# Three layers of a two-block transformer step in another order

## The chip, the cores and the metric

The kernel runs on one core of one Trainium2 chip. The metric is the device time of one execution in microseconds (us). Engines are named as the profile names them: PE (TensorE), PEld (its weight loads), DVE (VectorE), ACT (ScalarE), POOL (GpSimd), SP (SyncE, which only issues transfers here).

## What is computed

256 tokens of width 1024 go through two blocks, all in float32. Cut to what matters:

```
x = x + sliding_window_attention(norm(x))     # "SWA": 16 query heads, 4 key heads, window 128, sinks
x = x + swiglu_ffn(norm(x))                   # "FFN 1"
x = norm(x)
x = x + ab_mixer(norm(x))                     # "AB": a recurrence over tokens, both directions, 4 heads,
                                              #   beside a gated spatial mix, one output projection
x = x + relu2_ffn(norm(x))                    # "FFN 2a"
x = x + latent_attention(norm(x), positions)  # "MLA": 16 heads, low-rank queries and keys, rope
x = x + relu2_ffn(norm(x))                    # "FFN 2b"
return norm(x)

# the recurrence of one head and direction (h_fwd, h_bwd): out = num / max(|den|, exp(-m)),
# num and den from exp-weighted causal sums of q k v
ha = rms_norm(h_fwd + h_bwd, head_g) * sigmoid(o)
# the spatial mix: hb = gelu(u) * (rms_norm(gelu(v), v_g) mixed over tokens by ws, + bs)
# softmax attention of SWA: p = exp(s - m); out = (p / sum p) v
```

## The kernel before

All weights come as one stream of units of 128 x 1024 floats, two to a transfer of 1 MB (`raw`). Each unit is split before use into a high part (`wh`, ACT, line 262) and a rest (`wl`, DVE, line 263); activations are split in the same way (`hb`, `xb`: ACT lines 311 and 314, DVE lines 312 and 315). A product of two split operands is three matmuls: high with high, rest with high, high with rest. A unit is split when its turn in the program comes (`load`, by `self.ahead` and `self.limit`), and a transfer is issued when the buffer of the pair three before it has been read.

The code is written in program order, and a scheduler then sets each engine's queue by it; `high_priority`, `issue_after` and `keep_in_program_order` move single instructions. Each engine works through its queue in order, so an instruction that waits holds all behind it.

In SWA, pair j of heads goes through `proj(j)` (query projection), `soft(j)` (scores on PE; bias, maximum `swm`, exponentials, normalisation `sws` on DVE and ACT), `trans(j)` (the weights transposed on PE, copied to `swpt` by ACT) and `value(j)` (8 matmuls of 64 columns, then a split into `hb`). `out_steps` gives the output projection as steps (n, kp): column half n, and the k-th two pairs kp, 12 matmuls of 512 columns each. Steps (0, 0) to (0, 3) are interleaved with the last `trans` and `value` by `hooks`.

AB's recurrence (`ab_heads`) runs stages by a string: o (projection of the output gate), w (`weights`: decay by exp on ACT into `mex`, masked by POOL, times the scores on DVE), n (`numer`: numerator and denominator, `mden`, `mh`), b (projection of the spatial branch). ACT's functions come from several tables, and each change of table is an ACT_TABLE_LOAD. `uproj(m)` projects the third branch.

MLA projects to latents (`lck`, `lcq`), makes keys `kT` (`mla_keys`, two halves), queries per four heads (`rope(g)`, `nope(g)`), values (`values(n)`), and per head `soft(h)`, `trans(h)` (copy to `mpt`), and per two heads `value(j)`, which are laid out in a loop over heads, again with output steps among the last.

`boundary` adds the result to x and transposes it for the next stage (`x_trans`).

## Time and profile before

| | us |
|---|---|
| median of 3 runs (lowest to highest) | 849.87 (849.39 to 851.83) |
| the profiled execution, its own time | 851.47 |
| its span in the trace | 849.8 |
| SWA, to the first matmul of FFN 1 proper | 0 to 88.4 |
| AB, heads of the recurrence to its output projection | 317 to 362.9 |
| MLA, to the first matmul of FFN 2b | about 561 to 662.4 |

The span is what the trace covers, and the execution's own time holds 1.7 us around it. Times of day in the text (64.76) are us from the span's start.

### The profile page before, as it was taken

Reading aid. Unit: us, or ns where it says so; the run is one execution under the profiler, and the core shown is the slowest. Engines: PE = TensorE matmul, PEld = TensorE weight load, DVE = VectorE, ACT = ScalarE, POOL = GpSimd, SP = SyncE. Lnnn points to the kernel's source line nnn. Section 1 sums busy time; section 2 is a strip of 40 time slices with the busy share of each in tenths; the row PEclk is TensorE's granted clock in tenths of the full one; section 3 lists DMA queues with packets and bytes.
Section 4 is the critical chain, followed back from the end, with each engine's and each line's share of the span. In section 5 each row is a group of like instructions: output and inputs, shape, how many; then the busy total and the mean of one; then the engine's idle time right before and its main releaser. Section 6 shows DMA issues by size and latency. Waiting matters only on the chain.

```text
span 849.8 us, 12664 instructions
## 1 busy us (share of the span) xinstructions
PE 835.0 (98%) x4768; PEld 721.3 (85%) x4768; DVE 606.6 (71%) x1135; ACT 510.5 (60%) x972; POOL 41.5 (5%) x58
## 2 busy tenths in 40 slices
PE   9999999999999999999999999999999999999996
PEld 9877888888888987988888888898877888888885
DVE  5897776666766897787666766667878766666644
ACT  6696655555455969866455645456787744545532
POOL 0520000000000002200000000001000000000001
PEclk9999999999999999999999999999999999999999
DMA  9447555555554514554655555545217655555511
GB/s 328 173 163 263 179 208 191 196 180 179 196 199 148 199 51 149 199 205 148 220 184 195 195 198 197 195 169 173 85 51 245 219 206 199 198 184 175 190 47 49
DMA packets 24109, 151.41 MB, mean 178 GB/s; under 512 B 2768, under 2 KB 3536, under 8 KB 6768
## 3 DMA queue, kind: packets, MB, share of 16 engines
q1 hardware_dynamic: 23712, 149.95, 49.8%
q8 instruction: 37, 0.61, 0.3%
q10 hardware_dynamic: 288, 0.52, 0.2%
q0 software_dynamic: 48, 0.13, 0.1%
q14 instruction: 24, 0.20, 0.1%
HBM read 149.03 MB, written 1.05 MB: 177 GB/s over the span
## 4 chain that ended last, share of the span: by engine, by line
PE 78%; DVE 10%; ACT 6%; DMA 3%; issue 2%; POOL 1%; SPq 0%; POOLq 0%; DVEq 0%; ACTq 0%
PE ps L293 76%; DVE wl L263 3%; DMA raw<-in_w_dram 3%; PE ps L303 2%; ACT wh L262 1%; DMA x<-in_x_dram 1%; DVE qk L888 1%; DVE xb L315 1%; DVE sws L723 1%; ACT mpr L1291 1%; DVE sws L704 1%; ACT L890 0%; DVE qT L1259 0%; POOL r L319 0%; ACT mex L994 0%
## 5 line engine op out<-in xcount | busy, mean ns | idle before, releaser
L263 DVE TENSOR_TENSOR wl<-raw,wh 128x1024 fp32r<-128x1024 f32 (+4 forms) x278 | 329.3, 1190 | 134.8 <-ACT wh L262 128.9
L262 ACT ACTIVATE wh<-raw 128x1024 fp32r<-128x1024 f32 (+4 forms) x278 | 284.2, 1032 | 136.3 <-PE ps L293 123.0
L293 PE MATMUL ps<-xb,wh 128*128 128x512 f32 (+1 forms) x1304 | 283.5, 356 | 1.2 <-ACT wh L262 0.7
L293 PE MATMUL ps<-wh,hb 128*128 128x512 f32 (+1 forms) x944 | 280.3, 379 | 0.3 <-ACT hb L311 0.3
L293 PEld LDWEIGHTS ps<-xb,wh 128*128 128x128 f32 x1304 | 215.6, 189 | 32.9 <-DVE xb L315 1.6
L293 PEld LDWEIGHTS ps<-wh,hb 128*128 128x128 f32 x944 | 169.1, 189 | 31.9 <-issue 1.7
L293 PE MATMUL ps<-wl,hb 128*128 128x512 f32 (+1 forms) x472 | 177.6, 377 | 0.5 <-DVE wl L263 0.5
L293 PE MATMUL ps<-xb,wl 128*128 128x256 f32 x1084 | 159.3, 282 | 0.0
L293 PEld LDWEIGHTS ps<-xb,wl 128*128 128x128 f32 x1084 | 150.5, 191 | 9.4
L311 ACT ACTIVATE hb<-fp 128x256 fp32r<-128x256 f32 x90 | 36.9, 415 | 119.2 <-DVE fp L545 89.7
L293 PEld LDWEIGHTS ps<-wl,hb 128*128 128x128 f32 x472 | 88.8, 188 | 17.3 <-DVE wl L263 0.9
L312 DVE TENSOR_TENSOR hb<-fp,hb 128x256 fp32r<-128x256 f32 x90 | 37.7, 424 | 33.9 <-ACT hb L311 33.9
L447 DVE TENSOR_TENSOR fg<-ps,fg 128x256 f32<-128x256 f32 x108 | 44.6, 417 | 10.4 <-ACT fg L446 10.4
L446 ACT ACTIVATE fg<-ps 128x256 f32<-128x256 f32 x108 | 39.9, 369 | 11.1 <-PE ps L293 11.0
L293 PE MATMUL ps<-wh,xb 128*128 128x512 f32 (+3 forms) x192 | 39.8, 350 | 0.0
L293 PEld LDWEIGHTS ps<-wh,xb 128*128 128x128 f32 x192 | 31.6, 189 | 3.5
L319 POOL TENSOR_TENSOR r<-ms,mhalf 128x2 f32<-128x2 f32 x7 | 5.3, 760 | 485.4 <-DVE ms L324 485.4
L545 DVE SCALAR_TENSOR_TENSOR fp<-fg 128x256 f32<-128x256 f32 x64 | 26.8, 423 | 1.8
L314 ACT ACTIVATE xb<-ps,cols 128x256 fp32r<-128x256 f32 x35 | 15.5, 470 | 18.8 <-PE ps L303 12.9
L315 DVE SCALAR_TENSOR_TENSOR xb<-ps,cols,xb 128x256 fp32r<-128x256 f32 x35 | 16.0, 479 | 9.6 <-ACT xb L314 9.5
L293 PE MATMUL ps<-wl,xb 128*128 128x512 f32 (+3 forms) x96 | 21.4, 348 | 0.0
L1291 ACT ACTIVATE mpr<-ps,mnm,qsc 128x256 f32<-128x256 f32 x32 | 17.8, 574 | 4.3 <-DVE mnm L1287 4.2
(224 smaller groups left out, 611.0 us busy)
## 6 DMA issues: line engine op xcount, KB each, us to landing
raw<-in_w_dram SPq DMA_DIRECT2D x135, 1024.0 KB, 4.7
raw<-in_w_dram SPq DMA_DIRECT2D x4, 512.0 KB, 7.2
xraw<-in_xt_dram SPq DMA_DIRECT2D x4, 257.0 KB, 4.9
raw<-in_w_dram SPq DMA_DIRECT2D x4, 256.0 KB, 5.6
x<-in_x_dram SPq DMA_DIRECT2D x4, 256.0 KB, 6.5
row_fn<-in_fn_dram SPq DMA_DIRECT2D x2, 512.0 KB, 6.2
kT<-kr SPq DMA_DIRECT2D x1, 512.0 KB, 4.6
out_dram<-fo SPq DMA_DIRECT2D x2, 256.0 KB, 2.0
```

The lines of the kernel that those rows point to most:

```text
L262: a = self.nc.scalar.activation(hi[:, c], raw[:, c], AF.Copy)
L263: b = self.nc.vector.tensor_tensor(out=lo[:, c], in0=raw[:, c], in1=hi[:, c].bitcast(F32), op=ALU.subtract)
L293: self.nc.tensor.matmul(out, lhsT, rhs, start=start, stop=stop)
L303: self.nc.tensor.transpose(out, in_, self.ident)
L311: self.last_act = nc.scalar.activation(hi, src, AF.Copy)
L312: self.last_dve = nc.vector.tensor_tensor(out=lo, in0=src, in1=hi.bitcast(F32), op=ALU.subtract)
L314: self.last_act = nc.scalar.activation(hi, src, AF.Copy, scale=scale)
L315: self.last_dve = nc.vector.scalar_tensor_tensor(out=lo, in0=src, scalar=scale, in1=hi.bitcast(F32), op0=ALU.mult, op1=ALU.subtract)
L446: self.nc.scalar.activation(out, ps[:, T:], AF.Copy)
L447: self.nc.vector.tensor_tensor(out=out, in0=ps[:, :T], in1=out, op=ALU.add)
L545: nc.vector.scalar_tensor_tensor(out=p, in0=g, scalar=0.0, in1=g, op0=ALU.max, op1=ALU.mult)
L1291: nc.scalar.activation(pr[:, t], s3[:, t], AF.Exp, scale=qsc[:, t : t + 1], bias=nm[:, t : t + 1], accum_out=den[:, t : t + 1])
```

## The change

Three layers are reordered. In SWA, values are taken in twos (0 and 1 after `soft(4)`, 2 and 3 after `soft(6)`, and so on), there are six buffers `swpt` in place of four, and the end is written as `late`, with the step (1, 0) of the second column half ahead of values 6 and 7. In AB, sigmoid, exponentials and gelu wait for the last function of the table before (`issue_after`), the gate comes after w3, the multiplication by `head_g` goes from POOL into the split of `hh`, parts of `weights` and `numer` get priority, and `uproj(3)` is ahead of the transposes. In MLA, queries' `rope(0)` and `nope(0)` come ahead of the second half of the keys, values in twos after heads 7, 11 and 15, the weight units are split earlier and more evenly over the heads (`split`), and the end is again a `late` with steps of both column halves. The order of units in the stream follows.

```diff
@@ order of the output weights in the stream
+SWA_OUT = ((0, 0), (0, 1), (0, 2), (1, 0), (0, 3), (1, 1), (1, 2), (1, 3))
+MLA_OUT = ((0, 0), (0, 1), (1, 0), (0, 2), (1, 1), (0, 3), (1, 2), (1, 3))
...
@@ second_weights: latent attention
+            u.append(keys[0])
             for g4 in range(4):
...
                 if g4 == 0:
+                    u.append(keys[1])
                     u += wv
...
@@ def swa
-                pt = self.t([P, 3 * P], "swpt", 4)
+                pt = self.t([P, 3 * P], "swpt", 6)
...
-        hooks = {
-            1: lambda: (trans(6), value(5)),
-            2: lambda: (trans(7), value(6)),
-            3: lambda: value(7),
-        }
-        steps, accs = self.out_steps(acts, hooks)
+        steps, accs = self.out_steps(acts, {})
         for i in range(8):
             self.ahead = max(3, i - 1)
             proj(i)
@@ -761,14 +765,27 @@
                 soft(i - 1)
             if i >= 3:
                 trans(i - 3)
-            if i >= 4:
+            if i in (5, 7):
+                value(i - 5)
                 value(i - 4)
-        steps[0].pop(0)()
+        steps[0][0]()
         soft(7)
         trans(5)
-        value(4)
         self.pin = False
-        return self.boundary(steps, accs, lambda: None, nextw)
+
+        def late():
+            steps[0][1]()
+            trans(6)
+            value(4)
+            value(5)
+            steps[0][2]()
+            trans(7)
+            steps[1][0]()
+            value(6)
+            value(7)
+            steps[0][3]()
+
+        return self.boundary(([late], steps[1][1:]), accs, lambda: None, nextw)
...
@@ the ab layer
-        self.hg = self.row("hg")
...
-            nc.scalar.activation(y, y, AF.Silu)
+            self.last_silu = nc.scalar.activation(y, y, AF.Silu)
...
-        nc.scalar.activation(em, ac[:, :, 64:100], AF.Exp, scale=-1.0)
+        with self.tc.issue_after(self.last_silu.ins):
+            nc.scalar.activation(em, ac[:, :, 64:100], AF.Exp, scale=-1.0)
...
+                with self.tc.issue_after(self.last_silu.ins):
+                    for b, c0, cw, _, cb in segs:
+                        self.last_exp = nc.scalar.activation(exf[:, c0 : c0 + cw], bp[:, cb : cb + cw], AF.Exp, scale=-1.0, bias=ac[:, b, rr : rr + 1])
...
-                for b, c0, cw, cs, _ in segs:
-                    nc.vector.scalar_tensor_tensor(out=exf[:, c0 : c0 + cw], in0=sps[:, cs : cs + cw], scalar=P ** -0.5, in1=exf[:, c0 : c0 + cw], op0=ALU.mult, op1=ALU.mult)
+                with self.tc.high_priority(PRIO):
+                    for b, c0, cw, cs, _ in segs:
+                        nc.vector.scalar_tensor_tensor(out=exf[:, c0 : c0 + cw], in0=sps[:, cs : cs + cw], scalar=P ** -0.5, in1=exf[:, c0 : c0 + cw], op0=ALU.mult, op1=ALU.mult)
...
+                with self.tc.high_priority(PRIO):
+                    den = self.t([P, 2], "mden", 4)
...
-                nc.scalar.activation(o, ops[t], AF.Sigmoid, scale=r[:, t : t + 1])
-                nc.gpsimd.tensor_tensor(out=o, in0=o, in1=self.hg, op=ALU.mult)
+                with self.tc.issue_after(self.last_exp.ins):
+                    self.last_gate = nc.scalar.activation(o, ops[t], AF.Sigmoid, scale=r[:, t : t + 1])
...
-        for st in "o0 w0 o1 w1 o2 o3 n0 w2 b0 n1 w3 b1 n2 b2 n3 b3".split():
+        for st in "o0 w0 o1 w1 o2 o3 n0 w2 b0 n1 w3 g0 b1 n2 b2 n3 b3".split():
...
-                if u == 3:
-                    gate()
+            elif st[0] == "g":
+                gate()
...
-            nc.scalar.activation(gv, bps[t].rearrange("p (a b) -> p a b", a=4), AF.Gelu_apprx_tanh, scale=r[:, t : t + 1])
+            with self.tc.issue_after(self.last_gate.ins):
+                nc.scalar.activation(gv, bps[t].rearrange("p (a b) -> p a b", a=4), AF.Gelu_apprx_tanh, scale=r[:, t : t + 1])
...
-        for m in range(3):
+        for m in range(4):
             uproj(m)
+        hg = self.col("head_g", 4)
...
-                acts.append(self.split(ps[:, q * T : q * T + T], None, "h", 8))
+                k = hp * 2 + q
+                with self.tc.high_priority(PRIO):
+                    acts.append(self.split(ps[:, q * T : q * T + T], hg[:, k : k + 1], "h", 8))
...
-            if m >= 3:
-                uproj(m)
...
@@ def mla_heads
-        self.mla_keys(ckT, kT, 1)
...
-            pt = self.t([P, 2, T], "mpt", 3)
+            pt = self.t([P, 2, T], "mpt", 4)
...
-        steps, accs = self.out_steps(acts, {1: lambda: trans(14), 2: lambda: (trans(15), value(6)), 3: lambda: value(7)})
+        steps, accs = self.out_steps(acts, {})
         self.pin = True
         first = self.used
         self.limit = first + 7
         self.ahead = WBUFS
+
+        between = {
+            0: (lambda: values(0),),
+            1: (lambda: rope(1), lambda: values(1)),
+            2: (lambda: nope(1),),
+            4: (lambda: rope(2),),
+            5: (lambda: nope(2),),
+            8: (lambda: rope(3),),
+            9: (lambda: nope(3),),
+            10: (steps[0][0],),
+            13: (steps[0][1],),
+        }
+        split = {1: 1, 2: 1, 5: 1, 6: 1, 7: 1, 9: 1, 11: 1, 13: 1, 14: 1, 15: 1}
         rope(0)
         nope(0)
-        values(0)
+        self.mla_keys(ckT, kT, 1)
         for h in range(NH):
-            self.limit = first + 7 + min(h, 3) + (h >= 9) + (h >= 13)
+            self.limit += split.get(h, 0)
             self.load()
             soft(h)
+            if h in (7, 11, 15):
+                value((h - 7) // 2)
+                value((h - 5) // 2)
             if h >= 3:
                 trans(h - 3)
-            if h == 0:
-                values(1)
-            if h in (0, 4, 8):
-                rope(h // 4 + 1)
-            if h in (1, 5, 9):
-                nope(h // 4 + 1)
-            if h >= 5 and h % 2 == 1:
-                value((h - 5) // 2)
-            if h == 10:
-                steps[0].pop(0)()
+            for f in between.get(h, ()):
+                f()
         trans(13)
         self.limit = 1 << 30
         self.pin = False
         self.ahead = 4
-        return steps, accs
+
+        def late():
+            steps[1][0]()
+            trans(14)
+            value(6)
+            steps[0][2]()
+            trans(15)
+            steps[1][1]()
+            value(7)
+            steps[0][3]()
+
+        return ([late], steps[1][2:]), accs
```

DVE, end of SWA's softmax; `hb` is the rest of a value's split, `wl` of a weight unit, `swnm` the negative maximum of the last pair, `sws` its weights. Before, from the last `ISA` on:

```order
L704 ISA sws_947,swm_948<-ps_942,swb_951 128x128
L704 ISA swm_948 128x1
L312 TENSOR_TENSOR hb_992<-ps_987,hb_992 128x256
L707 SCALAR_TENSOR_TENSOR swnm_957<-swm_948,row_sinks_126 128x4
L263 TENSOR_TENSOR wl_1034<-raw_746,wh_1033 128x1024
L709 TENSOR_TENSOR swds_959<-swnm_957,row_sinks_126 128x4
L263 TENSOR_TENSOR wl_1072<-raw_837,wh_1071 128x1024
L717 TENSOR_TENSOR swden_961<-swden_961,swes_962 128x4
L263 TENSOR_TENSOR wl_1098<-raw_837,wh_1097 128x1024
L719 RECIPROCAL swrec_969<-swden_961 128x4
L312 TENSOR_TENSOR hb_1018<-ps_1013,hb_1018 128x256
L723 TENSOR_SCALAR sws_947<-sws_947,swrec_969 128x256
```

After, the same place:

```order
L272 TENSOR_TENSOR wl_1034<-raw_746,wh_1033 128x1024
L718 TENSOR_TENSOR swds_959<-swnm_957,row_sinks_126 128x4
L272 TENSOR_TENSOR wl_1064<-raw_829,wh_1063 128x1024
L726 TENSOR_TENSOR swden_961<-swden_961,swes_962 128x4
L272 TENSOR_TENSOR wl_1098<-raw_829,wh_1097 128x1024
L728 RECIPROCAL swrec_969<-swden_961 128x4
L321 TENSOR_TENSOR hb_1022<-ps_1017,hb_1022 128x256
L732 TENSOR_SCALAR sws_947<-sws_947,swrec_969 128x256
L732 TENSOR_SCALAR sws_947<-sws_947,swrec_969 128x128
L732 TENSOR_SCALAR sws_947<-sws_947,swrec_969 128x256
L732 TENSOR_SCALAR sws_947<-sws_947,swrec_969 128x128
L321 TENSOR_TENSOR hb_1030<-ps_1025,hb_1030 128x256
```

The split of value 4 (`hb_992` before, `hb_1022` after) stood ahead of the last pair's `swnm`, and now stands behind three weight units and the last pair's reciprocal; that of value 5 (`hb_1018`, now `hb_1030`) stands behind that pair's four `sws`.

ACT, AB, from the exponentials of head 1 on (`mden` is the denominator of head 0). Before:

```order
L262 ACTIVATE wh_3613<-raw_3511 128x1024
L262 ACTIVATE wh_3677<-raw_3511 128x1024
L1033 ACT_TABLE_LOAD
L1033 ACTIVATE og_3545<-ps_3445,r_3104 128x512
L1033 ACTIVATE og_3548<-ps_3446,r_3104 128x512
L1015 ACTIVATE mden_3555<-ps_3551 128x2
L1015 ACTIVATE mden_3569<-ps_3565 128x2
L262 ACTIVATE wh_3723<-raw_3601 128x1024
L1020 ACTIVATE mhf_3560<-ps_3551,mrec_3558 128x128
L1020 ACTIVATE mhf_3574<-ps_3565,mrec_3572 128x128
```

After:

```order
L1012 ACTIVATE mex_3503<-ps_3492,gac_2916 128x256
L271 ACTIVATE wh_3719<-raw_3593 128x1024
L271 ACTIVATE wh_3763<-raw_3593 128x1024
L271 ACTIVATE wh_3827<-raw_3603 128x1024
L271 ACTIVATE wh_3860<-raw_3603 128x1024
L1035 ACTIVATE mden_3547<-ps_3543 128x2
L1035 ACTIVATE mden_3561<-ps_3557 128x2
L1012 ACTIVATE mex_3579<-ps_3574,gac_2916 128x256
L1012 ACTIVATE mex_3579<-ps_3574,gac_2916 128x128
L1012 ACTIVATE mex_3585<-ps_3574,gac_2916 128x128
L1012 ACTIVATE mex_3585<-ps_3574,gac_2916 128x256
L1040 ACTIVATE mhf_3552<-ps_3543,mrec_3550 128x128
```

The gate's table load and its two `og` have gone from between, and `mden` now stands behind four `wh` where it stood behind two and the gate. Over the whole of AB there are 11 table loads on ACT before and 6 after, and 15 and 10 in the kernel.

PE, MLA, around the first two `value` blocks; `mpt,mlv` are the matmuls of a `value`, `kT,qT` those of a `soft`, `cols,mpr` those of a `trans`. Before:

```order
L293 MATMUL ps_6455<-mpt_6364,mlv_6145 64x256
L293 MATMUL ps_6455<-mpt_6386,mlv_6145 64x256
L293 MATMUL ps_6455<-mpt_6364,mlv_6146 64x256
L293 MATMUL ps_6455<-mpt_6386,mlv_6146 64x256
L293 MATMUL ps_6463<-kT_5812,qT_6253 128x256 x2
L303 MATMUL ps_6478<-cols,mpr_6351 128x128 x4
L293 MATMUL ps_6485<-kT_5812,qT_6253 128x256 x2
L303 MATMUL ps_6500<-cols,mpr_6373 128x128 x4
L293 MATMUL ps_6507<-mpt_6429,mlv_6145 64x256
L293 MATMUL ps_6507<-mpt_6483,mlv_6145 64x256
L293 MATMUL ps_6507<-mpt_6429,mlv_6146 64x256
L293 MATMUL ps_6507<-mpt_6483,mlv_6146 64x256
```

After:

```order
L302 MATMUL ps_6477<-kT_5808,qT_6248 128x256 x2
L302 MATMUL ps_6492<-mpt_6350,mlv_6099 64x256
L302 MATMUL ps_6492<-mpt_6372,mlv_6099 64x256
L302 MATMUL ps_6492<-mpt_6350,mlv_6100 64x256
L302 MATMUL ps_6492<-mpt_6372,mlv_6100 64x256
L302 MATMUL ps_6500<-mpt_6419,mlv_6099 64x256
L302 MATMUL ps_6500<-mpt_6471,mlv_6099 64x256
L302 MATMUL ps_6500<-mpt_6419,mlv_6100 64x256
L302 MATMUL ps_6500<-mpt_6471,mlv_6100 64x256
L312 MATMUL ps_6508<-cols,mpr_6359 128x128 x4
L302 MATMUL ps_6515<-kT_5808,qT_6374 128x256 x2
```

Values 0 and 1 stood apart, with a `soft` and a `trans` on each side; now they follow one another.

## Rows read from the trace of the kernel before

**Rows 1.** The page: span, and the busy time of the engines.

```profile
span 849.8 us, 12664 instructions
...
PE 835.0 (98%) x4768; PEld 721.3 (85%) x4768; DVE 606.6 (71%) x1135; ACT 510.5 (60%) x972; POOL 41.5 (5%) x58
```

**Rows 2.** The waits of PE: what ended them, us in total, times, longest.

```profile
PE ps L293 <- DVE mh L1021: 1.4, 1, 1.4
PE ps L303 <- DVE sws L723: 1.1, 1, 1.1
PE ps L293 <- issue: 0.6, 1, 0.6
PE ps L293 <- DVE mex L999: 0.6, 1, 0.6
PE ps L303 <- DVE mpr L1295: 0.6, 1, 0.6
PE ps L293 <- DVE xb L315: 0.5, 1, 0.5
PE ps L303 <- DVE xb L315: 0.5, 1, 0.5
PE ps L293 <- DVE wl L263: 0.5, 1, 0.5
PE ps L293 <- ACT hb L311: 0.3, 1, 0.3
```

**Rows 3.** Three stretches: busy us of each engine, granted clock, DMA.

```profile
44.00:71.70 27.70, 26.61 (x191) 20.90 (x191) 27.61 (x92) 25.34 (x67) 4.46 (x4) 1.00 0.57 203
317.00:336.00 19.00, 17.03 (x90) 14.24 (x89) 14.84 (x27) 18.86 (x33) 4.17 (x6) 1.00 0.46 166
610.00:640.00 30.00, 29.50 (x188) 22.77 (x187) 24.93 (x75) 25.33 (x73) 1.78 (x2) 1.00 0.13 44
```

**Rows 4.** Timeline of DVE, end of the sliding-window layer (start, us).

```profile
69.25 0.38 DVE L312 TENSOR_TENSOR hb<-ps,hb 128x256 fp32r<-128x256 f32 x1
...
69.56 0.99 DVE L723 TENSOR_SCALAR sws<-sws,swrec 128x256 f32<-128x256 f32 x4
...
70.47 1.21 DVE L263 TENSOR_TENSOR wl<-raw,wh 128x1024 fp32r<-128x1024 f32 x1
```

**Rows 5.** Timeline of PE, the same stretch and the next stage's start.

```profile
64.76 0.52 PE L303 MATMUL ps<-cols,sws 128*128 128x128 f32 x3 [1.09 <-DVE sws L723]
...
72.58 1.11 PE L293 MATMUL ps<-swpt,swv 128*64 128x256 f32 x8
...
88.37 0.39 PE L293 MATMUL ps<-xb,wh 128*128 128x512 f32 x1
```

**Rows 6.** Timeline of PE, heads 6 and 7 of the latent attention.

```profile
612.88 0.60 PE L303 MATMUL ps<-cols,mpr 128*128 128x128 f32 x4
613.32 1.03 PE L293 MATMUL ps<-kT,qT 96*128 96x256 f32 x4
614.18 0.60 PE L303 MATMUL ps<-cols,mpr 128*128 128x128 f32 x4
614.71 1.08 PE L293 MATMUL ps<-mpt,mlv 128*64 128x256 f32 x8
615.73 1.13 PE L293 MATMUL ps<-kT,qT 96*128 96x256 f32 x4
616.70 0.27 PE L303 MATMUL ps<-cols,mpr 128*128 128x128 f32 x1
```

**Rows 7.** Timeline of ACT, start of the recurrence's heads.

```profile
317.24 1.28 ACT L963 ACT_TABLE_LOAD   x1
```

**Rows 8.** Timeline of DVE, end of the AB layer.

```profile
357.71 1.66 DVE L1072 TENSOR_SCALAR gv<-gv,bbr 128x128 f32<-128x128 f32 x8 [1.76 <-POOL bbr L319]
...
361.89 0.42 DVE L312 TENSOR_TENSOR hb<-ps,hb 128x256 fp32r<-128x256 f32 x1
```

**Rows 9.** Timeline of PE, the AB layer's output projection begins.

```profile
362.85 0.40 PE L293 MATMUL ps<-wh,hb 128*128 128x512 f32 x1
```

More of the change, by code (lines that the diff above doesn't have):

```diff
@@ L53, in _pair_heads, with _out_units @@
     return 2 * p * 4 + g, (2 * p + 1) * 4 + g
-def _out_units(w):
-    return [_pa(w, 2 * kp, 2 * kp + 2, 512 * n, 512 * n + 512) for n in range(2) for kp in range(4)]
+PLAIN = tuple((n, kp) for n in range(2) for kp in range(4))
+SWA_OUT = ((0, 0), (0, 1), (0, 2), (1, 0), (0, 3), (1, 1), (1, 2), (1, 3))
+MLA_OUT = ((0, 0), (0, 1), (1, 0), (0, 2), (1, 1), (0, 3), (1, 2), (1, 3))
+def _out_units(w, order=PLAIN):
+    return [_pa(w, 2 * kp, 2 * kp + 2, 512 * n, 512 * n + 512) for n, kp in order]
 def _ffn_order(nf, nin):
@@ L82, in _weights @@
     rows = np.concatenate([_rng(h * 64, h * 64 + 64) for j in range(8) for h in _pair_heads(j)])
-    u += _out_units(w[rows])
+    u += _out_units(w[rows], SWA_OUT)
     wg, wd = i["ffn_w_gate_up"][0], i["ffn_w_down"][0]
@@ L113, in _weights @@
             w = i["c_w_ukv_2"][0]
+            keys = []
             for m in range(0, 8, 4):
-                u.append(np.concatenate([_pb(w, np.concatenate([_rng(h * P, h * P + 64) for h in (2 * a, 2 * a + 1)])) for a in range(m, m + 4)], 1))
+                keys.append(np.concatenate([_pb(w, np.concatenate([_rng(h * P, h * P + 64) for h in (2 * a, 2 * a + 1)])) for a in range(m, m + 4)], 1))
             vc = np.concatenate([_rng(h * P + 64, h * P + P) for h in range(NH)])
@@ L166, in _columns @@
     vec("v_g", i["ab_v_g_2"][0])
+    vec("head_g", i["ab_head_g_2"].reshape(-1))
     cw = i["ab_conv_2"][0].reshape(5, 2, 4, P).transpose(3, 2, 1, 0).reshape(P, 40)
@@ L1082, in uproj @@
             nc.vector.tensor_tensor(out=u0, in0=ps[:, :T], in1=rbc, op=ALU.mult)
-            u1 = self.t([P, T], "us", 3)
-            nc.scalar.activation(u1, u0, AF.Gelu_apprx_tanh)
+            u1 = self.t([P, T], "us", 4)
+            with self.tc.issue_after(self.last_gate.ins):
+                nc.scalar.activation(u1, u0, AF.Gelu_apprx_tanh)
             us[m] = u1
-        for m in range(3):
+        for m in range(4):
             uproj(m)
+        hg = self.col("head_g", 4)
         for hp in range(2):
@@ L1115, in mla @@
         qsc = self.t([P, 2], "qsc", 1)
+        self.k0 = self.t([32, T], "kr0", 1)
         self.swap = [(i + 16) % 32 for i in range(32)]
```

22 lines of the change are left out of this document (9 added, 13 removed).

## The prediction

> **What bounds the kernel now.** I read the page first: PE is busy 835.0 of 849.8 us [rows 1]. So the most that any order can bring back is what PE waits or wastes, and I read the waits of PE next [rows 2]. The reader is to see that they are few and single: each was one wait at one place. In SWA it is the transposes of pair 6, behind the normalisation `sws` (1.1 us). In AB they are the numerator behind `mex` (0.6), the scores of w3 behind `mh` of head 0 (1.4), and the spatial matmuls ("issue", 0.6). In MLA they are transposes behind `xb` (0.5), the transposes of head 1 behind `mpr` (0.6), the first output step behind a weight (0.5), the last behind `hb` (0.3), and the start of FFN 2b behind the last `xb` (0.5). Each costs somewhat more than its idle time, since the matmul ahead ends late by the model: the distance of the two starts is over that of its neighbours in the timeline by 1.25 (the transposes start at 64.76 [rows 5]), then 0.76, 1.53 and 0.80, then 0.66, 0.73, 0.67, 0.47 and 0.80. The sum is 7.7 us, which bounds the gain from waits.
>
> There is a second, smaller source. A `value` works in column halves of the array, and changing into and out of them costs [rows 6]: four transposes take 0.44 ahead of a `soft` (612.88 to 613.32), and 0.53 ahead of a `value` (614.18 to 614.71); a `soft` takes 0.86 (613.32 to 614.18), and 0.97 behind a `value` (615.73 to 616.70). That is 0.20 outside the block. Inside, 1.02 stands against 0.86 for its four pairs at the pace of a `soft`, 0.16 more, so a change in and out is worth up to 0.36. I take 0.34; below, 0.20.
>
> The third view is windows [rows 3]: who could take PE's place. Between 44.0 and 71.7 DVE is busy 27.61 of 27.70 us. This is the only stretch where another engine is fuller than PE, and the argument on SWA hangs on it.
>
> **The change, part by part.**
>
> SWA. The wait at the transposes goes (-1.25), and values in twos leave four changes of eight (4 x 0.34 = -1.36). But DVE's list until the rest of value 5 is the same in both orders, number for number. Before, this row starts at 69.25 and the four `sws` behind it end at 70.55 [rows 4]; after, it comes behind the four, so it ends at about 70.55 too, whatever PE does. What changes is what PE can do meanwhile. Before, it did step (0, 1), the last transposes and value 6 while DVE worked. After, the last pair's transposes stand behind step (0, 2), and the first half of (0, 2) needs value 4's split, which ACT has behind the last exponentials and DVE behind three weight units. PE gets there at 66.1 by the block lengths and stands until 69 or 70. From 70.55 it has left: a third of a step (0.9), the transposes (0.7), value 6 (0.8), and what before lies between value 7 at 72.58 and FFN 1 at 88.37 [rows 5], 15.79, less one change (0.34): 88.40, against 88.37. So even with DVE gapless SWA only comes out even. I add 0.7 for gaps in DVE's list: the denominator of pair 5 waits for its exponentials, now that no weight unit stands between (0.4), and 0.3 where splits wait on ACT. **SWA: +0.8**, from -0.2 (changes at 0.36, DVE a little ahead when the stretch begins) to +1.7 (gaps twice as long).
>
> AB. Five table loads of 1.28 us go [rows 7], most from the stretch ahead of n0, so `mex` is there in time: -0.76. The 1.4 at w3 is PSUM that `mh` of head 0 frees; after, `mden` stands behind four `wh` of 1 us each rather than two and the gate, the same length, and PE meets it one block earlier, in the second half of n1: 1.58 for 1.53 by the lists, +0.05 (bounds -1.5, if `mh` comes 1.5 earlier, as the gate's multiplication on POOL and its 2 us are gone; and +0.8). The wait at the spatial matmuls goes, as `uproj(3)`, 2.9 us long, now lies ahead and covers it: -0.80. PE would so be 1.5 ahead at the output projection, which begins at 362.85 [rows 9]. But its first split needs DVE, which before multiplies `gv` from 357.71, when POOL's `bbr` comes, for 1.66, and gives `hb` at 361.89 [rows 8]. After, gelu comes a little earlier and `gv` is done at about 356.4; then four weight units (1.14 each by the distance of starts) and three multiplications of `uproj` (0.33 each) stand ahead of the first `hb` (0.41): 362.4. PE begins at 362.4 or 362.5, not at 361.3. **AB: -0.4**, from -1.8 (no wait there, or none in n1) to +1.
>
> The table loads are the place for a rule of the Trainium skill, and it is a rival below. The page "ScalarE: Activation LUTs", section "Table sets: the hidden batching unit", says to batch calls by set of functions, with some 1.3 us for each load saved. By that price alone five loads would be 6.4 us; the trace has them on ACT, which is not the engine that ends last.
>
> The multiplication by `head_g` moves into a split, which costs DVE 4 x 0.06 and lies ahead of the projection while DVE waits for POOL: nothing. One transfer of 256 KB fewer: nothing, no wait there is a transfer's.
>
> MLA. The start gets worse. `rope(0)` and `nope(0)` need the splits of the latent queries, which the second half of the keys covered. By the same ACT and DVE rows PE waits 0.58, 0.41 and 0.18 for them where it waited 0.66: +0.5, and the first `soft` waits 0.2 for its rotated query. Further on there is more time between a `soft` and its transposes, and weights are split earlier, so four waits go: 0.73, 0.67, 0.47 and, at the start of FFN 2b, where wider matmuls of the first units now lie behind the transposes, 0.80: -2.67. Five runs of values for eight blocks: 3 x 0.34 = -1.0. Two new ones: value 1 needs `mpt` of head 3, which ACT has behind four `qT` and a weight unit (+0.3), and step (1, 0) takes PSUM that the exponentials of head 14 free, behind three weight units on ACT (+1.0; nothing if the units wait for their transfer behind them, 2 if in front). **MLA: -1.7**, from -3.3 (neither new wait) to +1.
>
> Sum: 0.8 - 0.4 - 1.7 = -1.3. The profiled execution took 851.47 with a span of 849.8, so it would take 850.2. It lies 1.6 above the median of the runs, which is the common measure: 849.87 - 1.3 = 848.6.
>
> **The rivals.**
>
> Faster by more: the new waits don't come. ACT and DVE reach their rows earlier, as the lists are compared by sums of durations that overlap. Then SWA is even (0), AB keeps its 1.8, MLA its 3.3: -5.1, 844.8. For it: each wait removed is measured, each new one only worked out. Against: the SWA bound is a sum of measured rows, and it alone takes back all that its part would gain. With half of that, 847.2, it is at the limit of what counts as faster.
>
> Slower: ACT becomes the bound in MLA's heads. Between 610 and 640 it is busy 25.33 of 30 us [rows 3], and PE's sum there is under 29 without its wait. After, four more weight units are split in the heads, 0.95 each: 29.1 of work. If the 4.7 us in which ACT stood for others stay, since exponentials follow maxima and copies follow transposes, the stretch takes 33.8, +3.8. The rest of MLA then gives +0.7 at its start and -0.73, -0.47 and -0.80 at the waits outside that stretch: +2.5, and with SWA and AB as above +2.9: 852.8. It makes the whole slower from 1.8 us of that idle time kept, and by over 0.3% from 4.3. Against: in my lists ACT is behind PE only at the two places priced above.
>
> The tables alone: the rule's 6.4 us all on PE's path, 843.5. Against it, PE's whole idle time in 317 to 336 is 1.97 [rows 3], so no more than that can come from them there.
>
> **How the numbers follow.** A measurement of this kernel tells apart about 0.3%, 2.5 us. My sum with its bounds (each part about 1 us to either side) has 0.57, and it ends within 0.3%: 848.6, itself between 847.4 and 850.2. The faster rival has 0.28, the tables 0.02, the slower 0.13. So faster 0.30, same 0.57, slower 0.13. The range goes to 845.4 below, where only the farther part of the faster rival is left out, and to 851.6 above, which leaves out the slower one from 3 us of kept idle time on; together about 0.2.
>
> **What would show it.** Right: no wait behind `sws` at transposes of pair 6, but a wait of 2.5 to 4 us in all at step (0, 2) of SWA behind `hb`; FFN 1's first matmul later than 88.4 by 0 to 1.7; 10 table loads; no wait behind `mex`; one of about 1.4 behind `mh` in n1; the output projection at about 362.5 plus what SWA shifted; four of MLA's waits gone, one by PSUM at step (1, 0). Wrong: PE enters SWA's (0, 2) without standing, so that SWA gains 2 us; MLA's new waits are missing or the heads' stretch gets longer by ACT; or AB's projection starts at 361.

## The result, and the profile after

| | us |
|---|---|
| kernel before, median of 8 runs (lowest to highest) | 849.80 (849.09 to 851.83) |
| changed kernel, median of 8 runs (lowest to highest) | 856.68 (852.92 to 857.53) |
| ratio, 95% interval | 1.0070 (1.0054 to 1.0086) |
| forecast | 848.6, range to 851.6 |

The change makes the kernel 0.7% slower, by 6.9 us. All eight runs lie above the forecast's range.

The page first, as in [rows 1]:

```profile
span 855.3 us, 12650 instructions
...
PE 837.3 (98%) x4768; PEld 725.0 (85%) x4768; DVE 608.2 (71%) x1135; ACT 504.7 (59%) x967; POOL 37.8 (4%) x56
```

PE has the same 4768 matmuls as before and is busy 2.3 us longer. So part of the loss is not in waits. The waits of PE, as in [rows 2]:

```profile
PE ps L302 <- ACT hb L320: 3.4, 1, 3.4
PE ps L302 <- DVE mh L1041: 1.6, 1, 1.6
...
PE ps L302 <- DVE hb L321: 0.9, 2, 0.5
PE ps L302 <- ACT mpt L1328: 0.9, 1, 0.9
PE ps L302 <- ACT mpr L1314: 0.9, 1, 0.9
PE ps L302 <- ACT kT L1244: 0.7, 1, 0.7
...
PE ps L302 <- ACT mex L1012: 0.4, 1, 0.4
PE ps L302 <- ACT xb L323: 0.4, 1, 0.4
```

The waits behind `sws` and `mpr` at transposes and behind `wl` have gone, as forecast. In their place stands one of 3.4 us behind `hb`, in SWA, and in MLA several that the forecast did not have or had smaller. Windows of SWA's end, of AB and of MLA's heads follow (busy us of PE, PEld, DVE, ACT, POOL, then granted clock, DMA share, GB/s). The last one holds the work that [rows 3] has at 610 to 640, which comes 4.9 us later here:

```profile
44.00:66.00 22.00, 21.54 (x168) 17.63 (x164) 21.15 (x78) 19.69 (x50) 4.33 (x4) 1.00 0.50 173
66.00:69.60 3.60, 0.22 (x5) 0.00 (x1) 3.52 (x7) 3.60 (x14) 0.00 (x0) 0.87 0.63 198
69.60:72.00 2.40, 2.40 (x6) 1.87 (x7) 2.40 (x9) 1.16 (x2) 0.00 (x0) 0.50 1.03 416
72.00:75.00 3.00, 3.00 (x9) 2.22 (x8) 0.64 (x1) 0.30 (x1) 0.00 (x0) 0.50 0.65 270
75.00:78.00 3.00, 3.00 (x17) 2.60 (x16) 1.23 (x1) 1.63 (x3) 0.00 (x0) 0.92 0.00 0
317.00:338.40 21.40, 19.36 (x101) 16.27 (x99) 21.09 (x42) 15.77 (x33) 3.13 (x6) 1.00 0.63 236
338.40:341.00 2.60, 2.60 (x9) 2.41 (x10) 2.21 (x8) 1.79 (x9) 0.00 (x0) 0.50 1.02 410
341.00:344.00 3.00, 3.00 (x15) 2.47 (x15) 0.69 (x3) 2.30 (x9) 0.41 (x1) 0.88 0.19 71
614.90:644.90 30.00, 28.58 (x180) 22.69 (x181) 27.51 (x75) 26.54 (x72) 1.56 (x2) 1.00 0.30 106
```

This view holds what the forecast missed. PE does nothing from 66.2 to 69.6, and when it works again its granted clock is 0.50, that is 1.2 in place of 2.4 GHz. It stays there until about 75.5 (the window of 75 to 78 has 0.92), with PE busy all the time. The same happens in AB, behind the wait in n1, from 338.4 on. The timeline of PE, as in [rows 5]:

```profile
64.70 1.52 PE L302 MATMUL ps<-swpt,swv 128*64 128x256 f32 x16
69.60 1.65 PE L302 MATMUL ps<-wh,hb 128*128 128x512 f32 x3 [3.38 <-ACT hb L320]
...
74.03 0.63 PE L302 MATMUL ps<-wh,hb 128*128 128x512 f32 x1
74.46 0.63 PE L302 MATMUL ps<-wl,hb 128*128 128x512 f32 x1
...
92.19 1.07 PE L302 MATMUL ps<-xb,wh 128*128 128x512 f32 x4
```

Two matmuls of 512 columns follow each other by 0.43 us (74.03 to 74.46). Before, the pace in the same step is 0.23 (75.10 to 75.33):

```profile
75.10 0.40 PE L293 MATMUL ps<-wl,hb 128*128 128x512 f32 x1
75.33 0.39 PE L293 MATMUL ps<-wh,hb 128*128 128x512 f32 x1
```

FFN 1 begins at 92.19, before at 88.37 [rows 5].

**Where the time went, by stage.** I measure each stage between the starts of the same two matmuls in each trace: SWA from its first scores to FFN 1's first matmul, AB from its first scores to MLA's first matmul (so with FFN 2a in it), MLA from there to the first down projection of FFN 2b. "Before" stands twice: the execution that the prediction worked with, and a second one (e5 below).

| trace | SWA | AB | MLA | time, median of the runs | before, same chip |
|---|---|---|---|---|---|
| before, as in the rows | 62.98 | 248.91 | 114.17 | 849.80 | |
| before once more (e5) | 62.99 | 248.85 | 112.72 | 850.02 (1) | 849.69 |
| changed | 66.97 | 249.97 | 114.55 | 856.68 | 849.80 |
| e1, SWA alone | 65.84 | 248.84 | 112.72 | 853.41 | 849.42 |
| e2, AB alone | 62.95 | 249.30 | 113.45 | 850.82 | 849.42 |
| e3, MLA alone | 62.99 | 248.89 | 114.39 | 851.38 | 849.42 |
| e4, e1 and PE kept at work | 64.54 | 248.89 | 112.67 | 852.00 | 849.42 |
| e6, e1 with a step in the wait | 61.91 | 249.08 | 113.30 | 849.81 | 849.69 |
| e7, e3 with three edits | 62.99 | 249.19 | 116.60 | 852.94 | 849.69 |
| e8, e2 with weights split later | 62.95 | 249.15 | 112.79 | 850.37 | 849.69 |
| e9, e3 with the start of before | 63.06 | 248.87 | 112.76 | 849.51 | 849.68 |
| e10, e3 with values one by one | 62.97 | 248.85 | 114.09 | 850.73 | 849.68 |
| e11, changed and PE kept at work | 64.59 | 249.32 | 114.51 | 853.76 | 849.68 |
| e12, the best of these together | 61.89 | 248.93 | 112.77 | 849.35 | 849.91 |

The stretch between SWA and AB, which no edit touches, is equal in all traces within 0.15 us. What lies behind MLA is not: it takes 171.5 to 171.7 in ten of the traces, and 172.2 in e1, e4, e6 and e12. Those 0.7 us lie behind PE's last matmul, where ACT issues a store of the result (`out_dram`) before its last operation: the issue takes 1.12 to 1.49 in these four and 0.37 or 0.38 in the others. In e5 and e1:

```profile
843.37 0.37 ACTq L1365 DMA_DIRECT2D out_dram<-fo  x1
```

```profile
845.79 1.12 ACTq L1378 DMA_DIRECT2D out_dram<-fo  x1
```

All four have SWA's new order with AB as before; why this lengthens the issue is not shown.

Against e5 the changed kernel loses 3.98 in SWA, 1.12 in AB and 1.83 in MLA. That is 6.9 in all, the difference of the medians.

The eight runs agree with the reading of the clock. Five of them, the profiled one included, 856.5 to 857.5, have a mean granted clock of 0.991, and three have 0.995, 0.997 and 0.999 with 855.1, 854.7 and 852.9. The kernel before has 0.997 to 0.999 throughout.

### The profile page after: what moved, and what is told of

It reads as the page before. It is cut to its first block, busy times and chain, and to the rows that moved or that the text cites. A ratio compares the mean times of both kernels' runs of the same rounds, so it can differ in the third digit from the quotient of the medians.

```text
span 855.3 us, 12650 instructions
## 1 busy us (share of the span) xinstructions
PE 837.3 (98%) x4768; PEld 725.0 (85%) x4768; DVE 608.2 (71%) x1135; ACT 504.7 (59%) x967; POOL 37.8 (4%) x56
## 3 DMA queue, kind: packets, MB, share of 16 engines
HBM read 148.77 MB, written 1.05 MB: 175 GB/s over the span
## 4 chain that ended last, share of the span: by engine, by line
PE 80%; DVE 12%; ACT 4%; issue 2%; POOL 1%; DMA 1%; ACTq 0%; DVEq 0%; POOLq 0%
PE ps L302 78%; DVE wl L272 4%; PE ps L312 2%; DVE qk L904 1%; ACT sws L725 1%; ACT mpr L1314 1%; DVE qT L1282 1%; DVE mmx L1309 1%; DVE mpr L1318 1%; DMA raw<-in_w_dram 1%; ACT wh L271 0%; DVE sws L732 0%; DVE xb L324 0%; DVE sws L713 0%; DVE mex L1018 0%
```

## The experiments

**The three parts apart (e1, e2, e3).** Each is the kernel before with one layer's part of the change, and with its order of units in the stream where that part has one:

```diff
 e1: only this
+SWA_OUT = ((0, 0), (0, 1), (0, 2), (1, 0), (0, 3), (1, 1), (1, 2), (1, 3))
+        def late():
...
 e2: only this
-        for st in "o0 w0 o1 w1 o2 o3 n0 w2 b0 n1 w3 b1 n2 b2 n3 b3".split():
+        for st in "o0 w0 o1 w1 o2 o3 n0 w2 b0 n1 w3 g0 b1 n2 b2 n3 b3".split():
...
 e3: only this
+MLA_OUT = ((0, 0), (0, 1), (1, 0), (0, 2), (1, 1), (0, 3), (1, 2), (1, 3))
+            if h in (7, 11, 15):
+                value((h - 7) // 2)
+                value((h - 5) // 2)
...
```

> The kernel before with the change in SWA alone. Theory A (PE stands 3.4 us behind the last values' splits, and the granted clock then stays at half for some 5 us): the first matmul of FFN 1 at 92.0 to 92.4, with 1.2 to 1.4 us of the +3.8 from the order itself and 2.4 to 2.6 from the clock, and a time of 853 to 854, where runs in which the clock does not fall come out near 851. Rival B (the loss is in the order alone): the same +3.8 in every run, whatever the clock shows. Rival C (the three layers act on each other): FFN 1 less than 1 us later, time within 0.3% of before.

> The kernel before with the change in AB alone. Theory A: PE stands about 1.8 us in the second half of n1 behind the first head's sums, the clock then falls to half for some 3 to 4 us, and the output projection begins about 1.1 us later than 362.85; in runs without the fall it is about 0.3 earlier than before. Time 850 to 851. Rival B (AB is as forecast, the clock falls there only because SWA's end came late): clock at full, time 849.4 or so. Rival C (AB is what costs most): over 852.

> The kernel before with the change in MLA alone. Theory A: the new waits (0.8 at the first scores, 1.3 in value 1, 0.7 at scores of a later head, 1.1 at step (1, 0)) give back what the removed waits and the values in twos bring, the clock stays full: FFN 2b's start +0.4, time 850.0 to 850.4, no difference that can be measured. Rival (MLA is as forecast, the waits come from a shifted start): -1.7, 848.1. Rival C (ACT bound): over 852.

Measured, as ratio to before: SWA 1.0046 (1.0033 to 1.0060), AB 1.0014 (1.0005 to 1.0023), MLA 1.0021 (1.0012 to 1.0030). The medians are 4.0, 1.4 and 2.0 above before, 7.4 together, against 6.9 for the whole. Each part is a loss by itself. That the sum fits is partly luck: by the traces, SWA is 1.1 and AB 0.7 longer in the changed kernel than alone, while e1 has 0.7 at the end of the kernel and e2 0.7 in MLA that the changed kernel has not.

In e1 the clock is low again behind the wait, in the trace and, by the mean of 0.996 in each, in all five runs. SWA is 2.9 longer than before and not 3.8, as the expectation had it, since the clock is back sooner (e4). AB alone has n1's wait, 1.85 us, and its clock stays full; its stage is 0.45 longer. In its MLA, which is before's, the profile shows a late weight transfer (ACT waits 1.67 for it at 647.79), and the stage is 0.73 longer than in e5. MLA alone came out above what theory A gave it, since A was measured against the execution in the rows (114.17) and not against e5 (112.72).

**PE kept at work in the wait (e4).** On e1:

```diff
             value(5)
+            spare = self.ps()
+            for _ in range(13):
+                self.mm(spare, acts[0][0][:, :P], acts[0][2])
             steps[0][2]()
```

> As e1_swa, with 13 matmuls of 512 columns (3.0 us at full clock) put on PE where it stands, ahead of step (0, 2); nobody reads what they write, so this only keeps PE at work in the wait. Theory A: the wait for the splits stays where it is (step (0, 2) at about 69.6), the granted clock stays at 1.00 behind it, the 512-column matmuls take 0.23 in place of 0.43, FFN 1 begins at about 89.8 in place of 92.2, and the time is 2.4 us below e1_swa, in all runs. Rival B (the slow matmuls come from something else than PE's standing): no change to e1_swa, or worse by what the 13 overrun.

The windows of e4 at the same place, and its timeline of PE:

```profile
66.00:69.60 3.60, 3.43 (x14) 2.25 (x12) 3.60 (x8) 3.60 (x15) 0.00 (x0) 1.00 0.64 207
69.60:72.00 2.40, 2.32 (x10) 1.94 (x11) 2.40 (x7) 0.52 (x1) 0.00 (x0) 1.00 1.01 420
72.00:75.00 3.00, 3.00 (x18) 2.52 (x17) 1.23 (x2) 1.82 (x3) 0.00 (x0) 1.00 0.46 194
```

```profile
65.69 3.24 PE L299 MATMUL ps<-hb 128*128 128x512 f32 x13
68.95 0.49 PE L299 MATMUL ps<-wh,hb 128*128 128x512 f32 x1
69.68 0.50 PE L299 MATMUL ps<-wh,hb 128*128 128x512 f32 x1 [0.23 <-DVE hb L318]
```

The useful work begins at the same time as in e1 (68.95 for 69.04), since the splits come when they come. But the clock is 1.00 behind it, the next 5.4 us hold 28 matmuls in place of 15 in the changed kernel, and SWA is 1.30 shorter than in e1. The medians differ by 1.4. The expectation had 2.4. In e1's trace the clock is back by 73, in the changed kernel's only at about 75.5, and the shorter fall costs less. Theory A holds in its mechanism, not in its size; that 13 matmuls whose results nobody reads make the kernel faster leaves little room for B.

**Useful work in the wait (e6).** On e1, a step of the second column half, whose values are long there:

```diff
-    u += _out_units(w[rows], SWA_OUT)
+    u += _out_units(w[rows], MLA_OUT)
...
             value(5)
+            steps[1][0]()
             steps[0][2]()
             trans(7)
-            steps[1][0]()
+            steps[1][1]()
             value(6)
...
-        return self.boundary(([late], steps[1][1:]), accs, lambda: None, nextw)
+        return self.boundary(([late], steps[1][2:]), accs, lambda: None, nextw)
```

> SWA alone as in e1_swa, but step (1, 0), whose values are long there, goes ahead of step (0, 2) into the wait, and (1, 1) takes its place. Theory A (SWA lost by PE standing 3.4 us and by the clock after it): the wait shrinks to under 1 us, the clock stays at 1.00, and FFN 1 begins 4.0 us earlier than in e1_swa, 1.2 earlier than in the kernel before; time 848.0 to 848.6. Rival B (DVE's list alone sets the end, as the forecast's bound says): the clock stays full, but the values 6 and 7 then wait for it, FFN 1 begins no earlier than before: 849.2 to 850.

SWA is 3.93 shorter than in e1 and 1.08 shorter than before, and the clock stays full:

```profile
66.00:69.60 3.60, 3.21 (x13) 2.07 (x11) 3.60 (x7) 3.60 (x15) 0.00 (x0) 1.00 0.64 234
69.60:72.00 2.40, 2.25 (x10) 1.87 (x11) 2.40 (x8) 1.54 (x2) 0.00 (x0) 1.00 0.99 369
```

Theory A holds for the stage. Its time does not come: the median is 3.6 below e1, but level with before (ratio 0.9996, 0.9987 to 1.0005). The end of the kernel takes back 0.7 of the 1.08, as in e1 and e4, and this trace gives back 0.23 in AB and 0.58 in MLA, where a split comes late behind weights; both layers are as before in this kernel.

**The kernel before once more (e5).** No edit.

> The kernel before, unchanged, profiled once more, to see whether the waits that the forecast counted as removed are there in each execution. Theory A (the profiled execution of before was a slow one of its kind, and the waits behind weight splits in MLA's last output steps, 0.47, and behind the last split at FFN 2b's start, 0.80, are late weight transfers of that execution): a time of 849.0 to 849.8, span near 847.6, and both waits missing, as they are in e1_swa and e4_swa_fill, where MLA is the same code. Rival: the waits are there at the same size, and the execution differs elsewhere.

Its time was 850.02, the profiled one of the rows 851.47. The difference is in MLA, 114.17 and 112.72. The two waits, behind ACT's `hb` and behind `xb` on L293 [rows 2], are not there. The timeline of ACT shows why: it splits a weight unit late, because the transfer lands late, and `hb` is queued behind. First in the trace of the rows, then in e5:

```profile
647.70 1.06 ACT L262 ACTIVATE wh<-raw 128x1024 fp32r<-128x1024 f32 x1 [1.53 <-DMA raw<-in_w_dram]
648.66 0.36 ACT L311 ACTIVATE hb<-ps 128x256 fp32r<-128x256 f32 x1
```

```profile
647.15 1.06 ACT L263 ACTIVATE wh<-raw 128x1024 fp32r<-128x1024 f32 x1 [0.95 <-DMA raw<-in_w_dram]
648.12 0.36 ACT L312 ACTIVATE hb<-ps 128x256 fp32r<-128x256 f32 x1
```

Theory A holds in its mechanism, though the execution is 0.2 above the time that it gave. One detail of it was loose: the first of the two waits is behind `hb`, and only through it behind a weight. Five more traces have before's MLA. The first wait stands in one of them (e2) and the second, at 0.40 in place of 0.80, in another (e6); e1, e4 and e8 have neither.

**MLA: its start (e9), its twos (e10), and three edits at once (e7).** All on e3:

```diff
 e9
-            u.append(keys[0])
+            u += keys
...
+        self.mla_keys(ckT, kT, 1)
         rope(0)
         nope(0)
-        self.mla_keys(ckT, kT, 1)
+        values(0)
...
 e10
-            if h in (7, 11, 15):
-                value((h - 7) // 2)
-                value((h - 5) // 2)
             if h >= 3:
                 trans(h - 3)
+            if h >= 5 and h % 2 == 1:
+                value((h - 5) // 2)
...
 e7
+        self.mla_keys(ckT, kT, 1)
         rope(0)
         nope(0)
-        self.mla_keys(ckT, kT, 1)
...
+            for j in {7: (0,), 8: (1,), 11: (2, 3), 15: (4, 5)}.get(h, ()):
+                value(j)
```

In e7 the order of units and `u += keys` are as in e9, and `split` lacks its entries for 14 and 15 too. In e9 `values(0)` and `values(1)` each come one place earlier in `between`.

> MLA alone as in e3_mla, with the start of before: both halves of the keys, then the latent queries, the first half of the values, then the first scores. Theory A (a third of MLA's loss is at the start, where queries ahead of keys wait 0.63, 0.34 and 0.86 against 0.40 and 0.66 before): 0.8 us below e3_mla, about 850.6, with the wait of 1.29 in value 1, 0.65 at later scores and 1.12 at step (1, 0) as they were. Rival (the start is a wash, the later waits shift with it): as e3_mla within 0.3.

> MLA alone as in e3_mla, with values one by one after every second head as before, but its start, split of weights and end as changed. Theory A (two values at a time cost more in waits, 1.29 and 0.65, than the 1.0 that three changes of the array's halves are worth): 0.9 below e3_mla, about 850.5, and the two waits gone. Rival B (the price of a change is higher than 0.34): no gain or a loss against e3_mla.

> MLA alone as in e3_mla, with three edits, each at one of its waits: keys ahead of latent queries again (start), value 1 one head later, and the last two weight units split after the exponentials of heads 14 and 15. Theory A (e3 loses by these waits, each on its own): the 0.86 at the first scores, the 1.29 in value 1 and the 1.12 at step (1, 0) go, 0.3 comes back for one more change into column halves, the lcq wait of before (0.66) returns; about 2.5 below e3, 848.6 to 849.2. Rival B (ACT's load in the heads is the cause): the waits show up a few steps later, time as e3 within 0.7 us.

e9 is 1.63 shorter in MLA than e3 and 1.9 in the median: with the start of before, nearly the whole loss of the layer goes. The waits of e3 at the start, in the timeline of PE:

```profile
584.24 0.39 PE L302 MATMUL ps<-xb,wh 128*128 128x256 f32 x1 [0.39 <-ACT xb L323]
...
585.40 0.44 PE L312 MATMUL ps<-cols,lcq 128*128 128x128 f32 x2 [0.18 <-DVE xb L324]
...
592.03 1.10 PE L302 MATMUL ps<-kT,qT 96*128 96x256 f32 x4 [0.70 <-ACT kT L1230]
```

In e9 one wait is left of these, 0.43 ahead of the transposes of `lcq`. Theory A had the direction, but only half of the size. The start itself brings what A gave it and a little more: value 0 begins 48.14 behind the layer's first matmul (611.85), in e3 49.13 (612.85). Value 1's wait, which stays and grows, takes 0.6 of this 1.0 back. Then the wait of 0.65 at later scores is gone, and the one at step (1, 0) is 0.5 shorter. That these two follow from the earlier start is argued, since e9 changes nothing else; through what they do is not shown.

e10 has values one by one and is 0.3 shorter than e3 in the stage. Its median is 1.05 above its before, e3's is 1.96 above its own, so 0.9 less, as theory A had it. The waits of 1.29 and 0.65 are replaced by smaller ones of 0.38 and 0.64 at its own values, and three more changes of halves eat the rest. So values in twos bring here what their waits cost, or a little less; the stage and the medians differ by 0.6 on how much less.

e7 comes out 1.6 above e3, where theory A had it 2.5 below. With the keys ahead and no `values(0)` behind `nope(0)`, nothing covers the rotation of the queries on DVE (`qr`, `qT`, 589.6 to 593.0). PE stands 2.2 us at the first scores, and the granted clock of 591 to 594 and of 594 to 597 is 0.70 and 0.73: value 0 begins 2.4 later than in e3. It is the same mistake as the one in SWA, made in an experiment. Value 1's wait and the one at step (1, 0) do go. But the wait at scores behind `hb` grows from 0.49 to 1.16, and one of 0.40 comes at another value, so at the layer's end only 0.2 is left of what they bring: there B was right. The timeline of PE in e7:

```profile
589.90 0.28 PE L301 MATMUL ps<-xb,wh 128*128 128x256 f32 x1
592.24 2.05 PE L301 MATMUL ps<-kT,qT 96*128 96x256 f32 x4 [2.06 <-issue]
```

**AB with weights split later (e8).** On e2:

```diff
                 if u == 0:
-                    self.ahead = 4
                     bps.extend((self.ps(), self.ps()))
+                if u == 1:
+                    self.ahead = 3
...
             acts.append(self.split(p, None, "h", 8))
+        self.ahead = 4
         return acts
```

> AB alone as in e2_ab, but weight units are split two ahead in place of four until b1 and three ahead from there to the end of the spatial mix, so that the first head's sums don't stand behind four of them. Theory A (the 1.85 us wait in n1 is these units on ACT and DVE): the wait goes to under 0.4. Of the 1.85 the output projection gives back what its first splits then lack, 0.5 to 1.5; time 0.4 to 1.4 below e2_ab: 849.4 to 850.4. Rival B (the sums wait for something else on their way): n1's wait stays at 1.5 or more, time as e2_ab.

n1's wait is 1.45 in place of 1.85 and the one ahead of it 0.72 in place of 0.48, so nothing is won there. ACT still has four `wh` ahead of `mden`, so the edit did not do what it was made for, and it does not decide between A and B. ACT also waits 0.86 for a transfer among these four. The traces add one thing for A: `mden` is through on ACT at about 330.1 in both, but on DVE three `wl` stand ahead of its next operation (331.24 in e2, 331.19 in e8) and a fourth ahead of its reciprocal, `mrec` (332.94 and 332.69), for which ACT's `mhf` waits 1.78 and 1.39. The end of n1's wait is thus DVE's queue more than ACT's. The median is 0.7 above its before, where e2 was 1.4 above; the traces differ mostly by the late transfer in MLA that e2's has and this one has not (113.45 against 112.79).

**The changed kernel with PE kept at work (e11).** The 13 matmuls of e4, in the changed kernel.

> The changed kernel with the 13 unread matmuls of e4_swa_fill in SWA's wait. Theory A (the clock falls twice in the changed kernel, 2.5 us lost in SWA and 1.3 in AB, and the one in AB follows from its own waits): 2.4 below the changed kernel, 854.2, with the clock still at half behind n1 and at full in SWA. Rival B (AB's fall is an echo of SWA's): no fall at all, 3.5 to 4 below, 852.8.

853.76, 2.9 below the changed kernel. SWA is 2.38 shorter and the clock full. In AB the same two waits stand in n1 (0.52 and 1.83), but the clock stays at 1.00 behind them, and the stage is 0.65 shorter. The windows of e11 in SWA and behind n1's wait:

```profile
69.00:72.00 3.00, 2.70 (x11) 1.78 (x10) 3.00 (x9) 1.55 (x4) 0.00 (x0) 1.00 0.92 385
335.00:338.00 3.00, 2.08 (x15) 2.01 (x16) 2.99 (x11) 2.24 (x9) 0.00 (x0) 1.00 0.98 396
338.00:341.00 3.00, 3.00 (x17) 2.49 (x16) 0.93 (x5) 2.66 (x11) 0.41 (x2) 1.00 0.36 142
```

By the clock B is nearer: with SWA's fall gone, AB's is gone too, in the profile and by the mean clock in four of five runs (0.998 and 0.999; the fifth has 0.995). By the time A is nearer (854.2 against B's 852.8), since AB's fall cost 0.65 and not 1.3. That one fall brings about the other is not shown by this.

**Together (e12).** SWA of e6, AB of before, MLA of e9 with value 1 one head later and without the last entry of `split`.

> What the runs point to, together: SWA as in e6_swa_cover (steps of the second column half in the wait), AB as before, MLA as in e9_mla_start with value 1 one head later and the last weight unit split after the exponentials. Theory A (each loss was one wait at one place): SWA gains 1.1 by FFN 1's start, MLA 0.4 by FFN 2b's as in e9 plus 1.0 for value 1's wait (1.39 less one change of halves) and 0.7 for the wait at step (1, 0): 2.5 to 3.2 in all, 846.5 to 847.2. Rival B (MLA's heads are close to ACT's and DVE's own pace, and a wait removed comes back some steps later): 1.0 to 1.5 in all, 848.2 to 848.7.

849.35 against 849.91, ratio 0.9994 (0.9985 to 1.0003): no difference that can be measured, and so no version here beats the kernel before. Both theories had more, A 2.5 to 3.2 and B 1.0 to 1.5. SWA keeps its 1.1, but the end of the kernel takes back 0.7 of it. MLA is at 112.77, just as before: value 1's wait has gone from 1.39 in e9 to 0.67 and the one at step (1, 0) is gone, but a wait of 0.39 came at another value, and two blocks whose halves start apart take 0.5 more. For MLA rival B's mechanism holds, a wait that is removed coming back some steps later.

## Why the prediction was wrong

The forecast's sum was -1.3 (0.8 - 0.4 - 1.7). Measured against e5 it is +6.9 (4.0 + 1.1 + 1.8). Of the difference of 8.2, SWA has 3.2, MLA 3.5 and AB 1.5.

**SWA, the step "so even with DVE gapless SWA only comes out even".** The wait itself was foreseen: PE "gets there at 66.1" and "stands until 69 or 70", and it stood from 66.2 to 69.60. What failed is the sum behind it. It took the work left from before's rows, at before's pace, as if a wait cost its own length only. PE came out of it at half clock, and that cost 2.4 us in the changed kernel (66.97 against 64.59 in e11). The prediction never asks what PE's clock does behind a wait; the longest ones it could look at, 1.25 and 1.53 us, had passed at full clock [rows 3]. The rest, +1.6 where +0.8 was forecast, is within its bounds.

The wait came about as stated, by both halves of value 4's split, though the bound goes by DVE alone. ACT's half ended it:

```profile
64.68 2.01 ACT L271 ACTIVATE wh<-raw 128x1024 fp32r<-128x1024 f32 x2 [0.85 <-DMA raw<-in_w_dram]
...
69.18 0.63 ACT L320 ACTIVATE hb<-ps 128x256 fp32r<-128x256 f32 x2
```

Between the two lines ACT is never idle, with the last pair's exponentials and copies. The 0.85 for a transfer ahead of them the forecast did not have; each trace with SWA's new order has 0.68 to 0.85 there, and the kernel before none. DVE's half came 0.7 behind ACT's, with four weight units between the last pair's maximum and it: the three of the forecast and one ahead of `swnm`. DVE's timeline in the changed kernel, as in [rows 4]:

```profile
64.85 1.22 DVE L272 TENSOR_TENSOR wl<-raw,wh 128x1024 fp32r<-128x1024 f32 x1
...
66.06 1.22 DVE L272 TENSOR_TENSOR wl<-raw,wh 128x1024 fp32r<-128x1024 f32 x1
...
67.27 1.22 DVE L272 TENSOR_TENSOR wl<-raw,wh 128x1024 fp32r<-128x1024 f32 x1
...
68.64 1.22 DVE L272 TENSOR_TENSOR wl<-raw,wh 128x1024 fp32r<-128x1024 f32 x1
...
69.87 0.39 DVE L321 TENSOR_TENSOR hb<-ps,hb 128x256 fp32r<-128x256 f32 x1
...
71.09 0.42 DVE L321 TENSOR_TENSOR hb<-ps,hb 128x256 fp32r<-128x256 f32 x1
```

The rest of value 5 ends at 71.5 and not at 70.55. The Trainium skill, page "TensorE: Matmul & The Clock Gate", section "HAM oscillation — how this bites in real kernels", tells of a kernel whose clock fell at each wait for data, and whose remedy was an order of work that keeps PE busy. e6 agrees with that: the same wait, filled with a step that was due anyway, made SWA 3.9 us shorter than e1. The page would have been the place to find this rival.

**MLA, the step "four waits go: 0.73, 0.67, 0.47 and ... 0.80".** They did go, but the last two were not in most executions: of the seven traces with before's MLA, four have neither (e1, e4, e5, e8). They came from weight transfers that landed late in the one profiled execution. The sum then took "1.6 above the median" off as well, so the same time was counted twice. This is 1.46 of the 8.2.

**MLA, the new waits.** The start was put at "+0.5" and "0.2" and cost 1.0 by the first value (e3 against e9): keys behind queries leave the copies of `kT` on ACT as the last thing ahead of the first scores. Value 1's wait for `mpt` of head 3, put at "+0.3", was 1.30, as ACT had four `qT` (1.57 together) and one `wh` (0.83) in front. A wait of 0.66 at scores (637.41) was not seen. "+1.0" for step (1, 0) was right: 1.12. These four are 0.3, 1.0, 0.66 and 0.1 over the forecast, 2.1 together, and with the 1.46 they make up MLA's 3.5. The price of 0.34 for a change of column halves fits the rows of after, where two values with the way out take 1.88 (633.08 to 634.96) against 2 x 1.02 [rows 6] for two alone, besides what lies outside the blocks. The term "-1.0" is thus right in size, and the waits of the twos take it back (e10).

**AB.** Forecast -0.4, measured +0.45 alone and +1.1 with the low clock. The waits at n0 (0.76) and at the spatial matmuls (0.80) went, as forecast. A new one of 0.48 behind `mex` stands at n1's first half, and n1's second half waits 1.85 for 1.58. All the same PE reaches the output projection earlier: 47.05 behind the first scores in e2 (361.79), before 47.69 (362.85 [rows 9]). The step that failed is "`gv` is done at about 356.4". The timelines of DVE and PE in e2, as in [rows 8] and [rows 9]:

```profile
355.38 1.66 DVE L1076 TENSOR_SCALAR gv<-gv,bbr 128x128 f32<-128x128 f32 x8 [1.75 <-POOL bbr L319]
...
362.55 0.48 DVE L315 SCALAR_TENSOR_TENSOR hb<-ps,cols,hb 128x256 fp32r<-128x256 f32 x1
```

```profile
363.08 0.50 PE L293 MATMUL ps<-wh,hb 128*128 128x512 f32 x1 [0.79 <-DVE hb L315]
```

In e2, where nothing else shifts it, `gv` ends 42.30 after the first scores (357.04 less 314.74); 356.4 would have been 41.24, so it is 1.06 late. It still waits for POOL, and the chain behind is as long as forecast (6.0). The rest of the first split comes so much later, and PE's projection starts with one matmul and then stands 0.8. That wait also took up part of the low clock's cost: PE stands 0.46 at the projection in the changed kernel, and 0.38 and 0.79 in e11. The fall cost the stage 0.65 (249.97 against 249.32 in e11), where the 3.3 us at half clock that the windows of 338.4 to 344 give would alone lose some 1.7, an estimate.

**The rivals.** The slower one, ACT as the bound of MLA's heads, is not what happened: ACT is busy 26.5 of 30 us at 614.9 to 644.9, where the rival's reckoning had 29. MLA lost at its start and at single waits. The tables: there are ten loads in place of fifteen, as forecast. PE's 0.76 at n0 went, which loads and order share in a way that no run tells apart, and the rest of the 6.4 us that they free on ACT does not show on PE's path: the stage is 0.45 longer. The 1.3 us for a load that stand with the rule in the prediction are the trace's, where each load takes 1.28 [rows 7]. The section of the Trainium skill that the prediction names with it has about 2.7 us for a load in its own example; the measurement decides.

**What stays open.** Why n1's wait brings the clock down in the changed kernel and not in e2 or e11, where the waits have the same length. Why the issue of the store at the end takes longer in four of the kernels. And why AB alone comes out at +1.4 by medians and +0.45 by its stage: e2's trace has a late transfer in MLA for the rest, but whether AB's part makes such transfers likelier, or they fell so in these runs, was not tried.

## What to carry to other kernels

A wait of PE costs its own length and, in some of the traces here, the clock behind it (2.4 us behind a wait of 3.4 in the changed kernel): where a change puts the stalls of several places into one, price the work after the wait at half speed as a rival, and look for independent work to put into it. Before counting a wait of the profile as a gain, see in a second execution that it is there; and don't correct to the median a time from which that wait has been taken already. Where DVE and ACT are nearly as full as PE, as at the end of SWA and, at 25 of 30 us, in MLA's heads, a better order for PE moves its waits about: the best four of twelve versions of these layers ended within 0.1% of before, the others behind it.
